# A one-core transformer block: bias tiles loaded in four groups, the position check moved to the table, one difference of the seven products on GpSimd, norm weights by a broadcast load

## The chip, the cores and the metric

The kernel runs on one core of a Trainium2 chip. The metric is device time in microseconds (us) of one execution; three runs of the kernel before gave a median of 908.03 us (907.3 to 908.68). Engines are called by the profile's names: PE is TensorE (PEld its weight loads), DVE is VectorE, ACT is ScalarE, POOL is GpSimd, SP is SyncE, which issues most DMAs. A name with a q (SPq, POOLq) is that engine's sequencer or its DMA queue.

## The reference: what is computed

One transformer block on x (512 x 1024, float32), with three mixers side by side, cut here to its skeleton:

```python
h = rms_norm(x, attn_norm)
proj = h @ w_in                                  # 1024 x 7176, split into 14 parts
o_a = dsa_attention(aq, ak, av, iq, ik, iw, positions, rel_bias)   # top-128 of an index score, T5 bias
o_b = hgrn2_mixer(bq, bf, bi, bg, lower_bounds, hgrn_out_norm)     # gated linear recurrence
o_c = mla_attention(q_nope, q_pe, k_nope, k_pe, v_c)               # causal attention, rope
mixed = g_a * (o_a @ w_up_a) + g_b * (o_b @ w_up_b) + g_c * (o_c @ w_up_c)   # g = sigmoid(gates)
x = x + mixed @ w_out
h = rms_norm(x, ffn_norm)
x = x + (silu(h @ w_gate) * (h @ w_up)) @ w_down # d_ff = 2816
return rms_norm(x, final_norm)
```

In `dsa_attention` a bias `rel_bias[t5_bucket(p_t - p_s)]` is added to the logits of query t and key s. It depends on positions alone. Where positions are consecutive it depends on t - s alone, and the kernel then takes it from a table of 640 distances.

## The kernel before, in words

**Numbers.** A float32 operand is split into two parts of a reduced type (fp32r): `hi` by a cast on ACT, `lo` by a subtraction on DVE, and each product is three matmuls, hi x hi, hi x lo and lo x hi (`mm3`, line 511). A weight tile (`unit`, line 485) is a load into one of three `raw` buffers by SP, a cast `whi` on ACT and a subtraction `wlo` on DVE.

**Products by seven.** The three gates and 18 of the 22 column blocks of the FFN (in pairs, for gate and up) go through `seven` (line 577): a product of a 1024 x 256 weight piece with the 512 columns of h, as 2 x 2 blocks by seven block products in place of eight (Strassen's scheme). It loads two `raw` tiles, the first with x11 and x21 and the second with x12 and x22, and makes four sums of them on DVE: s1 = x21 + x22, s3 = x11 - x21, s2 = s1 - x11, s4 = x12 - s2 (tiles named `sf`). Each of x11, x12, x22, s1, s3, s2 and s4 is split into `sh` and `sl` (`two`) and multiplied in 12 matmuls. It is called 30 times: 12 times for the gates (three branches of four units), 18 times in the FFN.

**Order.** The program text doesn't fix the order on the engines. Every instruction is put down as an `Op` of a `Plan` with its place in the text as its priority, and `Plan.run` (line 258) plays a list schedule ahead of time, with durations from `Plan.cost` (line 225). On each engine the op that can start earliest goes first, then the one with the lower priority number; SP's queue keeps the order of the text. For POOL `cost` takes 147 + 2.105 x n ns for an ordinary operation of n elements per partition, 1500 for a `branch`; a POOL load holds the queue for 1000. What comes out is one fixed order of instructions for each engine, with buffers assigned: among others 33 slots `g` of 128 x 512, three `raw`, eight PSUM banks. On the chip each engine runs its list in order and waits on semaphores for data and for buffers to come free. `plan.gate` (an op) makes later ops wait for that op in the plan; on the chip it is no wait, only a place in the list. `background` (line 938) gives ops a priority behind everything else.

**The start** (lines 451 to 479 and 551 to 572, 704 to 721). Eight warm-up matmuls of an identity run on PE. SP loads the first row tile of x (`xa`, `xb`), then the norm weights as two rows of 2 KB (`gra`, `grb`), then weights. PE broadcasts the rows over the partitions by a matmul with a row of ones, and DVE copies the result to `gna` and `gnb`. `norm_rows` takes the sum of squares of a row tile (for the first tile one half on ACT, one on DVE), its power -1/2 on POOL (`r`), `xn` = x * r * gain on DVE, transposes on PE, and `hT_hi` (ACT) and `hT_lo` (DVE). Four row tiles go by; behind each stands its share of the first projection (`cq`).

**Small loads and the check** (lines 723 to 767). SP loads masks, positions, `line` (0 to 511 on every partition) and small weights. `posr` is the positions as float. The check: the largest of posr - line and the largest of line - posr, each by one reduction over 512 elements on DVE (`jkp`, `ext`), and `odd` = whether they are not each other's negative, that is, whether positions are not consecutive.

**The bias** (lines 881 to 930, 994 to 1006). A matmul makes the table of 640 distances for four heads; POOL writes it to DRAM, `table`, then 128 copies of it, `skew`. `load_bias` reads 16 tiles from `skew` by POOL loads, for each query tile i and head one of 128 x 128(i+1), in the order i = 3, 2, 1, 0. Then a POOL `branch` loads `odd` into a register and computes the bias from the positions if it is set (lines 898 to 917); with the inputs here it is not. `block_mask` adds the causal or top-k mask in the background. All 16 loads and the branch are placed behind the end of the hgrn part (`hgrn_end`, line 1299).

**After that** come the three gated branches (`branch`, line 1270): 2 with `o_c`, 1 with `o_b`, then attention A, which reads the bias tiles, then 0 with `o_a`; each has four units with one call of `seven` and two sets of matmuls for the up-projection. Then the output projection, the FFN and the last norm.

Of the kernel before, what the change touches and what calls it, by code (L numbers as in the profile page):

```python
# [9 lines left out]
F32 = mybir.dt.float32  # L10
# [10 lines left out]
D = 1024  # L21
NF = 22
NG = 33
WARM = 8
PLAIN_GATES = ()
PLAIN = (0, 1, 2, 13)
SLACK = 500.0
# [373 lines left out]
def block_kernel(ctx: ExitStack, tc: tile.TileContext, x, positions, w_in, w_up_a, w_up_b, w_up_c, w_out, mla_q_norm,  # L401
# [25 lines left out]
    def const(shape, dt=F32, name="c"):  # L427
        v = plan.tile(nm("const"), shape, dt, name)
        slots[v.buf.cls] = [(cpool, v.buf.cls)]
        v.buf.left = 1  # L430
        return v
# [21 lines left out]
    P.affine_select(out=ident, in_=ident, compare_op=ALU.not_equal, fill=1.0, base=0, pattern=[[-1, 128]],  # L453
                    channel_multiplier=1)
    warm = bank("t")
    ones = const((128,), F32, "ones")
    P.memset(ones, 1.0)
    for _ in range(WARM):
        PE.matmul(warm[:, 0:128], ident, ident, start=True, stop=True)
    dpool = ctx.enter_context(tc.tile_pool(name="dpool", bufs=1, space=bass.MemoryType.DRAM))  # L460
# [7 lines left out]
    mhalf = const((8,), F32, "mhalf")  # L468
    P.memset(mhalf, -0.5)
    load_x(0)  # L470

    gn = (g(name="gna"), g(name="gnb"))
    gr = (g(name="gra"), g(name="grb"))
    for i in range(2):
        SP.dma_start(gr[i].part(0, 1), attn_norm[0:1, i * 512:(i + 1) * 512])
    for i in range(2):
        pg = bank("t")
        PE.matmul(pg, ones.part(0, 1), gr[i].part(0, 1), start=True, stop=True)
        V.tensor_copy(gn[i], pg)


    class W:
# [68 lines left out]
    def norm_rows(src, gain, dst, t, r=None, plain=None):  # L551

        if r is None:
            ss = st(2, "ss")
            for i in range(2):
                jk = g(name="jk")
                if i and not t and dst is hT:
                    V.tensor_tensor_reduce(out=jk, in0=src[i], in1=src[i], scale=1.0 / 1024, scalar=0.0, op0=ALU.mult,
                                           op1=ALU.add, accum_out=ss[:, i:i + 1])
                else:  # L560
                    A.activation(jk, src[i], AF.Square, scale=1.0 / 32, accum_out=ss[:, i:i + 1])
            r = rms2(ss, "r")
        tt = slice(t * 128, (t + 1) * 128)
        for i in range(2):
            xn = g(name="xn")
            V.scalar_tensor_tensor(xn, src[i], r, gain[i], op0=ALU.mult, op1=ALU.mult)
            pt = bank("t", (128, 4, 128))
            for k in range(4):
                PE.transpose(pt[:, k], xn[:, k * 128:(k + 1) * 128], ident)
            split_ps(dst[0][:, 4 * i:4 * i + 4, tt], dst[1][:, 4 * i:4 * i + 4, tt], pt)  # L570
            if plain:
                A.copy(plain[t // 2][:, 4 * i:4 * i + 4, (t % 2) * 128:(t % 2 + 1) * 128], pt)
# [4 lines left out]
    def seven(wsrc, c0, h, tsum, after=None):  # L577

        t1, t2, t3, t4 = tsum
        x = []  # L580
        for e in range(2):
            raw = plan.tile("raw", (4, 256), F32, "raw")
            SP.dma_start(raw, wsrc[512 * e:512 * e + 512, c0:c0 + 256].rearrange("(k p) c -> p k c", p=128))
            x.append([raw[:, :, 0:128], raw[:, :, 128:256]])

        def two(v):
            plan.gate = after
            hi = plan.tile("g", (4, 128), F32R, "sh", tag="sw")
            lo = plan.tile("g", (4, 128), F32R, "sl", tag="sw")
            A.copy(hi, v)  # L590
            V.tensor_sub(lo, v, f32(hi))
            plan.gate = None
            return hi, lo

        def add(method, a, b):
            plan.gate = after
            o = plan.tile("g", (4, 128), F32, "sf", tag="sf")
            getattr(V, method)(o, a, b)
            plan.gate = None
            return o  # L600

        def prod(o, wt, m, first=True, last=True):
            for k in range(4):
                mm3(o, wt[0][:, k], wt[1][:, k], m[0][:, k], m[1][:, k], first and k == 0, last and k == 3)

        def blk(k, t):
            return h[0][:, k, t], h[1][:, k, t]

        (x11, x21), (x12, x22) = x
        a, b, c = (bank("fs", (128, 2, 256)) for _ in range(3))  # L610
        d = bank("fs")
        prod(a[:, 0], two(x11), blk(ka, lo_t))
        p1 = g((128, 256), name="p1")
        A.copy(p1, a[:, 0])
        prod(a[:, 1], two(x12), blk(kb, lo_t))
        s1 = add("tensor_add", x21, x22)
        s3 = add("tensor_sub", x11, x21)
        s2 = add("tensor_sub", s1, x11)
        prod(b[:, 0], two(x22), t4)
        s4 = add("tensor_sub", x12, s2)  # L620
        prod(c[:, 1], two(s1), t1)
        prod(c[:, 0], two(s3), t3)
        prod(d[:, 0:256], two(s2), t2)
        p16 = g((128, 1, 256), name="p16")
        V.tensor_add(p16[:, 0], p1, d[:, 0:256])
        prod(b[:, 1], two(s4), blk(kb, hi_t))
        u = g((128, 2, 256), name="fu")
        V.tensor_add(p1, p1, a[:, 1])
        V.tensor_add(u, c, p16.to_broadcast([128, 2, 256]))
        o = g((128, 2, 256), name="fv")  # L630
        V.tensor_add(o, u, b)
        V.tensor_add(u[:, 0], u[:, 0], c[:, 1])
        return (p1, o[:, 1]), (o[:, 0], u[:, 0])
# [124 lines left out]
    V.tensor_copy(pos_f, pos_i)  # L758
    posr = g(name="posr")
    V.tensor_copy(posr, posr_i)  # L760

    ext = [const((1,), F32, "ext") for _ in range(2)]
    odd = const((1,), I32, "odd")
    jkp = g(name="jkp")
    for e, u, v in ((ext[0], posr, line), (ext[1], line, posr)):
        V.tensor_tensor_reduce(out=jkp, in0=u, in1=v, scale=1.0, scalar=-3e38, op0=ALU.subtract, op1=ALU.max, accum_out=e)
    V.scalar_tensor_tensor(odd, ext[0], -1.0, ext[1], op0=ALU.mult, op1=ALU.not_equal)
    sncs = g((128, 2, 4, 32), name="sncs")
    sn, cs = sncs[:, 0], sncs[:, 1]
    ang = g((128, 4, 32), name="ang")  # L770
# [110 lines left out]
    def load_bias():  # L881

        b3 = [g(name="bias3") for _ in range(4)]
        b20 = [g(name="bias2") for _ in range(4)]
        b1 = [g((128, 2, 256), name="bias1") for _ in range(2)]
        for h in range(4):
            bias[h, 3], bias[h, 2], bias[h, 0] = b3[h], b20[h][:, 0:384], b20[h][:, 384:512]
            bias[h, 1] = b1[h // 2][:, h % 2]
        keys = [(h, i) for i in (3, 2, 1, 0) for h in range(4)]
        for h, i in keys:  # L890
            S = 128 * (i + 1)
            first = TL * h + 511 - 128 * i
            P.dma_start(bias[h, i], View(skew.buf, np.arange(S), (
                lambda a, first=first, S=S: bass.AP(tensor=a.tensor, offset=a.offset + first,
                                                    ap=[[4 * TL - 1, 128], [1, S]]),)))
        scr = [g(name="scr") for _ in range(4)]

        def general(nc, odd, posr, pos_f, rb, *tiles):
            q = nc.gpsimd
            r = q.value_load(odd[0:1, 0:1])  # L900
            with tc.If(r != 0):
                for i in range(NT):
                    S = 128 * (i + 1)
                    d, w, e, u = (v[:, :S] for v in tiles[:4])
                    q.tensor_scalar(d, posr[:, :S], -1.0, pos_f[:, i:i + 1], op0=ALU.mult, op1=ALU.add)
                    bh = [t for t, k in zip(tiles[4:], keys) if k[1] == i]
                    for h in range(4):
                        q.tensor_scalar(bh[h], d, 1.0, rb[:, 0, h:h + 1], op0=ALU.is_lt, op1=ALU.mult)
                    q.tensor_scalar(w, d, float(BOUNDS[0]), None, op0=ALU.is_ge)
                    for k in range(1, 32):  # L910
                        if k < 31:
                            q.tensor_scalar(e, d, float(BOUNDS[k]), None, op0=ALU.is_ge)
                            q.tensor_tensor(w, w, e, op=ALU.subtract)
                        for h in range(4):
                            q.tensor_scalar(u, w, rb[:, k, h:h + 1], None, op0=ALU.mult)
                            q.tensor_tensor(bh[h], bh[h], u, op=ALU.add)
                        w, e = e, w

        plan.add([("Pool", "branch", (odd, posr, pos_f, rb), dict(
            body=general, outs=scr + [bias[k] for k in keys]))])  # L920

    def block_mask(i):
        S = 128 * (i + 1)
# [62 lines left out]
    for t in range(NT):  # L986
# [3 lines left out]
        A.copy(v, p)  # L990
        vc.append(v)


    rbk = const((4,), F32, "rbk")
    SP.dma_start(rbk.part(0, 32), rel_bias)
# [271 lines left out]

    mixed = [None] * 8

    def branch(n, wu, o, first):  # L1270
        wuu = None
        for u in range(4):
            if u % 2 == 0:
                wuu = unit([(wu[0][:, 256 * u:256 * u + 512], 0)], 4, 512)
            plain = n in PLAIN_GATES
# [20 lines left out]
                    V.tensor_mul(sg, sg, p)  # L1296
                    V.tensor_add(mixed[j], mixed[j], sg)

    plan.gate = hgrn_end
    load_bias()  # L1300
    plan.gate = None
    for i in range(NT):
        background(block_mask, i)
    branch(2, w_up_c, ocT, True)
    branch(1, w_up_b, obT, False)

    oaT = (o8(name="oa_hi"), o8(name="oa_lo"))
# [191 lines left out]
```

## Time and profile before

| | us |
|---|---|
| median of three runs | 908.03 |
| profiled execution | 913.61 |
| span of it, first to last instruction | 911.0 |
| mean granted PE clock | 0.994 |
| bytes moved by DMA | 90.36 MB, mean 99 GB/s |

A row of a timeline reads: start, length, engine, line, operation, tiles written <- tiles read, shapes, count, and in brackets the idle time of that engine before it and who ended it. L397 is the line at which the planned order is emitted, so nearly all instructions carry it and are told apart by their tiles. In a windows row stand the stretch, its length, busy time of PE, PEld, DVE, ACT and POOL (with the number of instructions), the granted PE clock, the share of the DMA engines in use and GB/s. A waits row gives who waited for whom: us in total, times, the longest.

### The profile page before, as it was taken

The page shows a single profiled execution, that of the slowest core. Times are in us where ns is not written, and L with a number is a line of the kernel's source. Part 1 is how long each engine was busy: PE and PEld are TensorE (multiplying, and loading weights), DVE is VectorE, ACT ScalarE, POOL GpSimd, SP SyncE. Part 2 cuts the span into 40 slices and gives each one's busy share as a digit, 9 for nine tenths or more (in the row PEclk, how much of TensorE's full clock was granted, in tenths as well). Part 3 has the DMA queues.
Part 4 walks back from the last instruction along what each step waited for, and adds up shares of the span by engine and source line. Part 5 has one row for each costly group of instructions (what it writes and reads, how often), then busy time and mean ns, then how long its engine had stood idle before and what let it go on. Part 6 is the DMA issues. An engine that isn't in the chain of part 4 may idle for free.

```text
span 911.0 us, 16024 instructions
## 1 busy us (share of the span) xinstructions
PE 890.6 (98%) x6304; PEld 795.1 (87%) x6304; DVE 673.7 (74%) x1382; ACT 440.5 (48%) x915; POOL 27.6 (3%) x51
## 2 busy tenths in 40 slices
PE   9899999999999899999999999999999999999997
PEld 7897878888788899998999878999999999988885
DVE  5566999968866797979649558789996899533335
ACT  6654687333535454537925347454454453422313
POOL 1000000000002200000000000000000000000000
PEclk9999999999999999999999999999999999999999
DMA  7343150333202632334104731323342334341312
GB/s 237 74 116 85 42 151 24 93 92 94 72 26 74 205 94 64 122 96 136 47 5 135 235 112 47 116 71 95 121 132 71 94 101 149 99 139 50 110 49 92
DMA packets 77920, 90.36 MB, mean 99 GB/s; under 512 B 8778, under 2 KB 64238, under 8 KB 77716
## 3 DMA queue, kind: packets, MB, share of 16 engines
q1 hardware_dynamic: 76596, 85.13, 30.8%
q0 software_dynamic: 1104, 3.94, 1.5%
q8 instruction: 49, 0.80, 0.4%
q14 instruction: 27, 0.22, 0.1%
q10 hardware_dynamic: 144, 0.26, 0.1%
HBM read 87.21 MB, written 3.42 MB: 99 GB/s over the span
## 4 chain that ended last, share of the span: by engine, by line
PE 79%; DVE 8%; DMA 7%; ACT 3%; issue 2%; SPq 0%; POOL 0%; POOLq 0%; ACTq 0%; DVEq 0%
PE ps L397 78%; DMA raw<-in_w_in 3%; DMA raw<-in_w_ffn_up 1%; DVE wlo L397 1%; PE ps L1089 1%; DVE sl L397 1%; DVE sf L397 1%; DMA line<-in_consts_f 1%; DMA x2b<-in_x 1%; DMA raw<-in_w_ffn_gate 1%; DVE fu L397 0%; ACT whi L397 0%; DVE quarters_sl L397 0%; DVE p L397 0%; DMA raw<-in_w_up_a 0%
## 5 line engine op out<-in xcount | busy, mean ns | idle before, releaser
L397 DVE TENSOR_TENSOR wlo<-raw,whi 128x1024 fp32r<-128x1024 f32 (+3 forms) x91 | 104.3, 1166 | 47.1 <-ACT whi L397 37.0
L397 ACT CAST whi<-raw 128x1024 fp32r<-128x1024 f32 (+3 forms) x91 | 89.2, 1006 | 56.7 <-DMA raw<-in_w_ffn_up 23.0
L397 PE MATMUL ps<-whi,hT_lo 128*128 128x512 f32 (+3 forms) x160 | 55.5, 349 | 2.3 <-DVE hT_lo L397 2.3
L397 PE MATMUL ps<-whi,hT_hi 128*128 128x512 f32 (+3 forms) x160 | 55.5, 352 | 1.3 <-ACT hT_hi L397 1.3
L397 ACT CAST sh<-sf 128x512 fp32r<-128x512 f32 x75 | 45.6, 619 | 22.7 <-DVE sf L397 19.7
L397 PE MATMUL ps<-wlo,hT_hi 128*128 128x512 f32 (+3 forms) x160 | 55.3, 347 | 0.0
L397 PE MATMUL ps<-hT_hi,wlo 128*128 128x512 f32 x136 | 54.5, 400 | 0.0
L397 PE MATMUL ps<-hT_hi,whi 128*128 128x512 f32 x136 | 54.3, 399 | 0.0
L397 PE MATMUL ps<-hT_lo,whi 128*128 128x512 f32 x136 | 54.1, 398 | 0.0
L397 PE MATMUL ps<-whi,quarters_ah 128*128 128x512 f32 x160 | 53.2, 389 | 0.0
L397 ACT CAST sh<-raw 128x512 fp32r<-128x512 f32 x55 | 33.1, 619 | 39.4 <-DMA raw<-in_w_ffn_gate 16.0
L397 PE MATMUL ps<-tl,sh 128*128 128x256 f32 x176 | 49.8, 283 | 0.0
L397 PE MATMUL ps<-th,sh 128*128 128x256 f32 x176 | 49.8, 283 | 0.0
L397 PE MATMUL ps<-th,sl 128*128 128x256 f32 x164 | 46.4, 283 | 0.0
L397 PE MATMUL ps<-whi,quarters_sl 128*128 128x512 f32 x120 | 40.0, 389 | 0.0
L397 PE MATMUL ps<-h_hi,sh 128*128 128x256 f32 x136 | 38.6, 284 | 0.0
L397 PE MATMUL ps<-h_lo,sh 128*128 128x256 f32 x136 | 38.5, 283 | 0.0
L397 PE MATMUL ps<-hth,sh 128*128 128x256 f32 x132 | 37.6, 286 | 0.0
L397 PE MATMUL ps<-htl,sh 128*128 128x256 f32 x132 | 37.5, 285 | 0.0
L397 PE MATMUL ps<-h_hi,sl 128*128 128x256 f32 x128 | 36.2, 283 | 0.0
L397 PEld LDWEIGHTS ps<-whi,hT_lo 128*128 128x128 f32 x160 | 31.4, 196 | 5.0 <-DVE hT_lo L397 2.6
L397 PEld LDWEIGHTS ps<-whi,hT_hi 128*128 128x128 f32 x160 | 31.3, 197 | 4.9 <-ACT hT_hi L397 2.2
(422 smaller groups left out, 2870.8 us busy)
## 6 DMA issues: line engine op xcount, KB each, us to landing
raw<-in_w_in SPq DMA_DIRECT2D x51, 512.0 KB, 3.7
raw<-in_w_ffn_down SPq DMA_DIRECT2D x22, 512.0 KB, 4.3
raw<-in_w_ffn_gate SPq DMA_DIRECT2D x18, 512.0 KB, 3.6
raw<-in_w_ffn_up SPq DMA_DIRECT2D x18, 512.0 KB, 4.2
raw<-in_w_out SPq DMA_DIRECT2D x8, 512.0 KB, 4.4
raw<-in_w_up_c SPq DMA_DIRECT2D x4, 512.0 KB, 3.7
raw<-in_w_up_b SPq DMA_DIRECT2D x4, 512.0 KB, 3.5
raw<-in_w_up_a SPq DMA_DIRECT2D x4, 512.0 KB, 3.7
```

The lines of the kernel that those rows point to most:

```text
L397: getattr(real[e], method)(*[fix(v) for v in a], **{n: fix(v) for n, v in k.items()})
L1089: nc.tensor.matmul(v[2 * n + i], v[i], v[n + i], start=True, stop=True)
```

## The change

Six edits. (1) `WARM`, the number of warm-up matmuls, goes from 8 to 11. (2) The norm weights come by two loads that read the 2 KB row once for each partition (256 KB each) in place of rows, ones, matmuls and copies. (3) The second square of the first tile goes from DVE to ACT. (4) In `seven`, s3 is made by POOL. (5) The position check goes from its place among the small loads to a place behind the MLA values `vc`, ahead of the table, gated there. (6) `load_bias` becomes a generator: the four loads of one i are placed behind whatever op was last put down before each unit of branch 2 (i = 3 ahead of unit 0, i = 0 ahead of unit 3), the POOL branch behind branch 2, and the masks after it.

```diff
 NG = 33
-WARM = 8
+WARM = 11
 PLAIN_GATES = ()
...
     warm = bank("t")
-    ones = const((128,), F32, "ones")
-    P.memset(ones, 1.0)
     for _ in range(WARM):
...
     load_x(0)
-
     gn = (g(name="gna"), g(name="gnb"))
-    gr = (g(name="gra"), g(name="grb"))
     for i in range(2):
-        SP.dma_start(gr[i].part(0, 1), attn_norm[0:1, i * 512:(i + 1) * 512])
-    for i in range(2):
-        pg = bank("t")
-        PE.matmul(pg, ones.part(0, 1), gr[i].part(0, 1), start=True, stop=True)
-        V.tensor_copy(gn[i], pg)
+        SP.dma_start(gn[i], bcast(attn_norm[0, i * 512:(i + 1) * 512], 512))
 
...
                 jk = g(name="jk")
-                if i and not t and dst is hT:
-                    V.tensor_tensor_reduce(out=jk, in0=src[i], in1=src[i], scale=1.0 / 1024, scalar=0.0, op0=ALU.mult,
-                                           op1=ALU.add, accum_out=ss[:, i:i + 1])
-                else:
-                    A.activation(jk, src[i], AF.Square, scale=1.0 / 32, accum_out=ss[:, i:i + 1])
+                A.activation(jk, src[i], AF.Square, scale=1.0 / 32, accum_out=ss[:, i:i + 1])
             r = rms2(ss, "r")
...
 
-        def add(method, a, b):
+        def add(method, a, b, eng=V):
             plan.gate = after
             o = plan.tile("g", (4, 128), F32, "sf", tag="sf")
-            getattr(V, method)(o, a, b)
+            getattr(eng, method)(o, a, b)
             plan.gate = None
...
         s1 = add("tensor_add", x21, x22)
-        s3 = add("tensor_sub", x11, x21)
+        s3 = add("tensor_sub", x11, x21, P)
         s2 = add("tensor_sub", s1, x11)
...
     V.tensor_copy(posr, posr_i)
-
-    ext = [const((1,), F32, "ext") for _ in range(2)]
-    odd = const((1,), I32, "odd")
-    jkp = g(name="jkp")
-    for e, u, v in ((ext[0], posr, line), (ext[1], line, posr)):
-        V.tensor_tensor_reduce(out=jkp, in0=u, in1=v, scale=1.0, scalar=-3e38, op0=ALU.subtract, op1=ALU.max, accum_out=e)
-    V.scalar_tensor_tensor(odd, ext[0], -1.0, ext[1], op0=ALU.mult, op1=ALU.not_equal)
     sncs = g((128, 2, 4, 32), name="sncs")
...
         keys = [(h, i) for i in (3, 2, 1, 0) for h in range(4)]
-        for h, i in keys:
+        for n, (h, i) in enumerate(keys):
+            if n % 4 == 0:
+                yield
             S = 128 * (i + 1)
...
                                                     ap=[[4 * TL - 1, 128], [1, S]]),)))
+        yield
         scr = [g(name="scr") for _ in range(4)]
...
             body=general, outs=scr + [bias[k] for k in keys]))])
+        yield
 
...
 
+    plan.gate = plan.ops[-1]
+
+    ext = [const((1,), F32, "ext") for _ in range(2)]
+    odd = const((1,), I32, "odd")
+    jkp = g(name="jkp")
+    for e, u, v in ((ext[0], posr, line), (ext[1], line, posr)):
+        V.tensor_tensor_reduce(out=jkp, in0=u, in1=v, scale=1.0, scalar=-3e38, op0=ALU.subtract, op1=ALU.max, accum_out=e)
+    V.scalar_tensor_tensor(odd, ext[0], -1.0, ext[1], op0=ALU.mult, op1=ALU.not_equal)
+    plan.gate = None
 
...
 
-    def branch(n, wu, o, first):
+    def branch(n, wu, o, first, between=None):
         wuu = None
         for u in range(4):
+            if between:
+                plan.gate = plan.ops[-1]
+                next(between)
+                plan.gate = None
             if u % 2 == 0:
...
 
-    plan.gate = hgrn_end
-    load_bias()
+    lb_ = load_bias()
+    next(lb_)
+    branch(2, w_up_c, ocT, True, lb_)
+    plan.gate = plan.ops[-1]
+    next(lb_)
     plan.gate = None
...
         background(block_mask, i)
-    branch(2, w_up_c, ocT, True)
     branch(1, w_up_b, obT, False)
...
```

## The prediction

> **What bounds the kernel now.** I read the page first, then TensorE's waits, then the windows around the two longest ones, then the timeline and the chain of waits inside them.
>
> ```profile
> span 911.0 us, 16024 instructions
> PE 890.6 (98%) x6304; PEld 795.1 (87%) x6304; DVE 673.7 (74%) x1382; ACT 440.5 (48%) x915; POOL 27.6 (3%) x51
> ...
> PE   9899999999999899999999999999999999999997
> ...
> DVE  5566999968866797979649558789996899533335
> ```
>
> TensorE (PE) is busy for 98% of the span. What a change can win is PE's idle time (911.0 - 890.6 = 20 us) and the stretches in which PE runs at half its clock. The longest waits of PE, by who ended them:
>
> ```profile
> PE ps L397 <- ACT sh L397: 2.7, 1, 2.7
> PE ps L397 <- DVE hT_lo L397: 2.3, 1, 2.3
> ```
>
> Both are single events, at 297 and 26.7 us. Windows laid around them (busy time of PE, PEld, DVE, ACT, POOL with instruction counts, then granted clock, DMA share, GB/s):
>
> ```profile
> 24.00:26.60 2.60, 2.00 (x13) 1.24 (x10) 0.22 (x2) 2.58 (x6) 0.00 (x0) 1.00 0.70 187
> 26.60:30.00 3.40, 1.08 (x7) 1.02 (x7) 3.28 (x9) 1.69 (x6) 0.00 (x0) 1.00 0.25 61
> 30.10:33.50 3.40, 3.40 (x13) 3.40 (x12) 2.85 (x15) 1.80 (x3) 0.00 (x0) 0.50 0.00 0
> 33.50:37.00 3.50, 3.50 (x22) 3.50 (x21) 0.69 (x3) 2.33 (x6) 0.00 (x0) 1.00 0.01 2
> ...
> 296.30:299.70 3.40, 1.00 (x5) 0.50 (x3) 0.57 (x2) 0.35 (x1) 0.00 (x0) 1.00 0.96 347
> 299.75:303.10 3.35, 3.08 (x11) 2.79 (x12) 3.35 (x7) 2.96 (x6) 0.00 (x0) 0.50 0.22 46
> ```
>
> Each gap is followed by 3.4 us at a granted clock of 0.50: the same kind of matmul goes through 13 times in 3.4 us, then 22 times in 3.5. So each event costs its gap and another 3.4 x 0.5 = 1.7 us: 2.3 + 1.7 = 4.0 us near 27, 2.7 + 1.7 = 4.4 us near 297. The Trainium skill, "TensorE: Matmul & The Clock Gate" (Part 1), describes the same free-running window of 3413 ns, but asks for an idle gap above about 3.4 us; here gaps of 2.3 and 2.7 us were followed by the drop, so the trace decides. By that rule each event would be worth its gap alone, and the sum below would come out some 2.5 us smaller.
>
> **The position check** (old lines 762 to 767). What holds PE at 26.7:
>
> ```profile
> 26.72 0.69 DVE L397 CUSTOM_DVE_ANT_0 jkp<-posr,line 128x512 f32<-128x512 f32 x1 [2.50 <-DMA line<-in_consts_f]
> ...
> 28.24 1.88 DVE L397 TENSOR_TENSOR hT_lo<-ps,hT_hi 128x512 fp32r<-128x512 f32 x3
> ...
> 28.98 0.45 PE L397 MATMUL ps<-whi,hT_lo 128*128 128x384 f32 x1 [2.31 <-DVE hT_lo L397]
> ```
>
> VectorE (DVE) runs in order. The check's first reduction waits 2.50 us for the load of `line`; behind it are queued the four splits `hT_lo` of the last two row tiles, and PE waits for the first. Moved behind the MLA values, the check no longer stands there, while `line` is loaded as before and has landed long since. The split could then go once ScalarE's `hT_hi` is there, whose own waits in this place are the 0.6 us that PE idles at 24 to 26.6. I take 4.0 us for gap and clock together, bounds 2.0 (the tile behind it is late for its own sake, and the clock still drops) and 4.6 (the 0.6 goes too). At its new place the check is two reductions of 0.69 us and a compare: about 1.5 us of DVE at 120 us, where DVE's strip reads 9 (slices 5 to 8, 91 to 182 us) and PE's reads 9 as well. What fills DVE there is mostly the top-k rounds, which the planner puts at the lowest priority and nobody waits for; if the check falls between a softmax's steps instead, it costs up to 1.5. I take +0.5.
>
> **Norm weights and warm-up** (old lines 455 to 479, 557). The start:
>
> ```profile
> 4.17 0.69 DVE L397 CUSTOM_DVE_ANT_0 jk<-xb 128x512 f32<-128x512 f32 x1 [4.17 <-DMA xb<-in_x]
> ...
> 5.30 0.55 POOL L397 TENSOR_TENSOR r<-ms,mhalf 128x1 f32<-128x1 f32 x1 [3.84 <-DVE ms L397]
> ...
> 6.42 0.83 ACT L397 CAST whi<-raw 128x768 fp32r<-128x768 f32 x1 [2.21 <-DMA raw<-in_w_in]
> ...
> 7.28 0.69 DVE L397 COPY gna<-ps 128x512 f32<-128x512 f32 x1 [2.14 <-PE ps L397]
> 8.08 0.75 DVE L397 SCALAR_TENSOR_TENSOR xn<-xa,r,gna 128x512 f32<-128x512 f32 x1
> 8.49 0.63 ACT L397 ACTIVATE jk<-xa 128x512 f32<-128x512 f32 x1 [0.24 <-DMA xa<-in_x]
> ...
> 10.68 0.69 PE L397 MATMUL ps<-whi,hT_hi 128*128 128x384 f32 x1 [0.68 <-ACT hT_hi L397]
> ```
>
> The factor `r` is there at 5.85, but `xn` starts at 8.08, after the broadcast matmuls and their copy. In their place come two loads of 256 KB, third and fourth in SyncE's queue. Between 4.17 and 8.49 there landed 384 + 384 + 256 KB (two weight tiles and `xa`): 237 KB per us. So the first half of the weights lands about 4.17 + 1.1 = 5.3 and `xn` can start at about 6.0 instead of 8.08. But everything behind the two loads lands 512 / 237 = 2.2 us later: the first weight tile at 8.6 instead of 6.4, cast by 9.4, so the first real matmul goes at about 9.4 instead of 10.68: a gain of 1.3 us, not 2.1. The square that moves from DVE to ScalarE ends at about 5 us as before (`xb` lands at 4.17, and a square takes ScalarE 0.63): nothing. The three more warm-up matmuls run while PE waits for `xn`: nothing, unless they bring the full clock a window sooner, for up to 1.7. What the extra 512 KB does after that:
>
> ```profile
> 9.60:13.00 3.40, 2.73 (x11) 2.20 (x11) 3.40 (x7) 2.35 (x5) 0.17 (x1) 1.00 0.37 92
> 13.00:16.40 3.40, 3.40 (x12) 3.40 (x11) 3.40 (x5) 1.81 (x5) 1.03 (x1) 1.00 0.89 302
> 16.40:20.00 3.60, 3.60 (x25) 3.52 (x25) 1.76 (x5) 3.33 (x10) 0.55 (x1) 1.00 1.08 370
> ```
>
> From 13 to 20 us the DMA engines are full, and the last rows of x come in there. From 9.6 to 13 they are 37% used, because SyncE waits for a weight slot: 0.63 x 3.4 = 2.1 us of room, about what the two loads take. I take -1.3, bounds -3.0 (a clock window too) and +2.2 (no room used).
>
> **Bias tiles in four groups** (old lines 881 to 920, 1299 to 1304). The wait at 297 is for a weight tile:
>
> ```profile
> 291.19 2.26 POOL L397 DMA_DIRECT2D bias<-skew  x4
> ...
> 305.41 0.55 POOL L397 DMA_DIRECT2D bias<-skew  x1 [9.54 <-PE ps L397]
> ```
>
> ```profile
> 292.39 6.88 DMA raw<-in_w_in
> ...
> 299.35 0.63 ACT sh L397
> ```
>
> ```profile
> raw<-in_w_in SPq DMA_DIRECT2D x51, 512.0 KB, 3.7
> ...
> bias<-skew POOLq DMA_DIRECT2D x4, 256.0 KB, 4.2
> ```
>
> That load took 6.88 us where the median of its kind is 3.7, with the DMA engines at 0.96: four bias loads of 256 KB and two of 192 KB stand beside it. Without any it would land at 296.1, before PE runs dry at 297.3. But the plan's gate only orders the queue: the first group, the four of 256 KB, is issued behind the last product of the branch before, and that is the same place. What goes for certain is the two of 192 KB, 384 KB at the window's 347 KB per us: 1.1 us of the gap. A gap of 1.6 in a window of 3.4 may or may not halve the clock. I take -2.0 (1.1 and half of 1.7), bounds 0 and -4.4.
>
> On GpSimd's queue the groups, and the branch behind them, now stand ahead of the differences of later units. A bias load waited 9.54 us there for a slot that PE held. The branch takes from its load of the flag to the instruction after it:
>
> ```profile
> L900 POOLq TENSOR_LOAD <-odd x1: 491/491/491, 315.5 to 315.5; - x1
> ```
>
> ```profile
> L901 POOLq EVENT_SEMAPHORE  x1: 17/17/17, 319.2 to 319.2; - x1
> ```
>
> some 3.8 us, in which a difference queued behind it cannot start, nor ScalarE's cast of it, nor PE's product. The planner counts 1.5. The slot waits follow PE's own progress, so what stands behind them isn't due sooner; I take +0.5 for both, bounds 0 and +2.3 (3.8 - 1.5).
>
> **The difference on GpSimd** (old line 617). It is `x11 - x21`, once for each of 30 products by seven: 12 in the branches, 18 in the FFN. On DVE in the FFN:
>
> ```profile
> 600.00:690.00 90.00, 88.93 (x737) 88.35 (x737) 85.99 (x158) 45.30 (x90) 0.00 (x0) 1.00 0.35 106
> ```
>
> ```profile
> L397 DVE TENSOR_TENSOR sf<-raw 128x512 f32<-128x512 f32 x8 | 5.5, 684 | 0.0
> ```
>
> ```profile
> PE ps L397 <- ACT p L397: 1.1, 2, 0.7
> PE ps L397 <- ACT whi L397: 0.8, 1, 0.8
> ```
>
> In these 90 us nine products go by: 84 matmuls each, 0.121 us a piece (88.93 / 737), so 10.1 us of PE, and 9.55 us of DVE (85.99 / 9). The change takes 0.68 from DVE, which leaves 8.9. But DVE isn't PE's limit yet: in the whole FFN PE waits 1.9 us (the third fence), and so no more than 1.9 can be won. What the difference takes on GpSimd no row shows. Nearest rows:
>
> ```profile
> L397 POOL TENSOR_TENSOR rb<-ms,mhalf 128x4 f32<-128x4 f32 x4 | 4.0, 1012 | 60.7 <-DVE ms L397 60.7
> ...
> L397 POOL MEMSET at<- 128x512 f32 x4 | 2.1, 526 | 96.2 <-DVE kT L397 70.9 <-ACT sm L397 15.7 <-PE ps L397 9.6
> ```
>
> A pass of the same size that only writes takes 0.53; two reads and a write would make three such passes, 1.6 as an estimate from that row. I take 1.2, between the two and the planner's own figure (line 256: 512 x 2.105 + 147 ns). GpSimd is free for it (3%), and its product is the fifth of the seven in the code, so four others, 4 x 12 x 0.121 = 5.8 us of PE, cover its lateness. I take -0.5, bounds -1.9 and, by the second rival, +12.
>
> **Sum.** -4.0 + 0.5 - 1.3 - 2.0 + 0.5 - 0.5 = -6.8 us. The profiled execution took 913.6 (span 911.0 and 2.6 around it), 5.6 more than the median of 908.0; the terms are waits that both have, so 906.8 profiled, and **901.2** as the median. Its own range, from the neighbouring bounds, is 897.5 to 904.5.
>
> **Rivals.** *The start is bound by its loads.* For it: 0.89 and 1.08 of DMA between 13 and 20 us. If the 512 KB does not fit into the free 2.1 us, the last rows of x come 2.2 us later, PE finds the gap again a little further on, and the clock drops again. The start then gives 0 instead of -5.3: 901.2 + 5.3 = 906.5.
>
> *The difference collides with DVE.* For it: DVE has only 10.1 - 8.9 = 1.2 us to spare in each FFN product, and 11 of its operations there read two SBUF tiles. If it is held while GpSimd reads, each difference costs DVE its length and the one operation that GpSimd itself waits for, 1.2 + 0.68 = 1.9 us; from 1.2 on DVE is the bound. That is 0.7 us x 18 = 12.6 us, less the 0.5 counted: 901.2 + 13 = 914; a half of it still gives 908. Against it: GpSimd is used 3% of the time in this trace, so no row shows a collision. The Trainium skill, "SBUF — State Buffer" (Who interferes with whom), does say that a DVE instruction with two SBUF inputs contends with a GpSimd instruction that reads SBUF, and that the second blocks until the first is done. By that rule the time would be this rival's 914; no row here tests it, which is why the rival has a chance of its own.
>
> *The groups change nothing*, since the first MB is issued at the same moment: the wait at 297 stays whole, 901.2 + 2.0 = 903.2, and the branch on GpSimd may take 1 more: 904.
>
> **How the numbers follow.** Forecast 0.60, loads 0.17, collision 0.13, groups 0.10. A measurement can tell about 0.2% from no change, 1.8 us: faster is below 906.2, slower above 909.8. The forecast and the last rival are faster; of the first rival 0.45 faster, 0.4 same, 0.15 slower; of the collision most is slower. Together 0.75 faster, 0.11 same, 0.14 slower. The range runs from 895 (start and wait both at their best bounds) to 910 (the collision at a third, or the loads with the check's cost); beyond it is what is left of the collision and of a reordered plan.
>
> **What would show it.** Right: PE has no wait above 1 us for `hT_lo` before 35 us, no half-clock stretch near 30, `xn` starts near 6.0 and the first product near 9.4; the raw load at the start of the first branch lands in 5 to 6 us. Wrong: DVE operations of 128x512 with two SBUF inputs well over 0.69 us in the FFN, `sf` on POOL over 1.7, PE waiting for `sh` there; or the same gap at 25 to 35 us ended by `xa` or `xb`.

## The result, and the profile after

Four runs of the changed kernel gave a median of 920.15 us (919.3 to 920.63), four of the kernel before beside it 908.36 (907.3 to 909.93): a ratio of 1.0127 with a 95% interval of [1.0110, 1.0145], so 11.8 us slower. 901.2 was forecast, with a range up to 910. The profiled execution took 919.3 us. The two profiled executions differ by 5.7 us only, because that of before lay 5.6 above its median and this one 0.9 below.

The head of its page and the strips of PE and DVE:

```profile
span 917.5 us, 16114 instructions
...
PE 890.1 (97%) x6306; PEld 794.8 (87%) x6306; DVE 671.3 (73%) x1348; ACT 443.1 (48%) x919; POOL 74.8 (8%) x80
...
PE   7899999999999999999999999999999999999997
...
DVE  4566999968866778987695468789897899542335
```

PE's busy time is as before (890.6), the span is 6.5 us longer: PE waits more. DVE lost 34 instructions (30 differences, the two copies, a square with its readout), which at 0.68 us should be some 23 us of busy time; it lost 2.4. POOL took 47 us more.

PE's waits (us in total, times, longest), the longest first:

```profile
PE ps L397 <- ACT p L397: 7.0, 7, 1.3
PE ps L397 <- DVE xn L397: 3.5, 3, 1.5
PE ps L397 <- ACT hT_hi L397: 2.2, 3, 1.0
PE ps L397 <- DVE hT_lo L397: 1.6, 1, 1.6
```

The wait of 2.7 for `sh` at 297 is gone from the top. The wait for `hT_lo` is still there, 1.6 us at 27, and in front is what stood at 1.1 us in two waits in the whole of before: `p`, a step of the products by seven.

The FFN window and windows around the start, with the columns of the windows before (busy time of PE, PEld, DVE, ACT, POOL; granted clock, DMA share, GB/s):

```profile
24.00:26.60 2.60, 1.82 (x16) 1.58 (x15) 1.59 (x9) 1.83 (x6) 0.00 (x0) 1.00 0.80 185
26.60:30.00 3.40, 1.78 (x7) 1.46 (x7) 3.26 (x10) 3.35 (x8) 0.00 (x0) 0.86 0.22 52
29.06:32.47 3.41, 3.41 (x12) 3.41 (x12) 2.02 (x8) 2.98 (x11) 0.00 (x0) 0.50 0.00 0
...
600.00:690.00 90.00, 86.06 (x709) 85.08 (x707) 81.98 (x146) 42.14 (x83) 11.77 (x8) 1.00 0.34 101
```

In 90 us of the FFN 709 matmuls go by where there were 737: 28 x 0.121 = 3.4 us lost, as an estimate. DVE is busy for 82 of the 90 us, less than before, so it isn't the bound by its load. POOL takes 11.77 us for 8 operations, 1.5 each.

The same operations by tile, with least, median and largest duration in ns. Before:

```profile
L397 DVE TENSOR_TENSOR sl<-sf,sh x39: 681/686/694, 286.5 to 772.9; 128x512 fp32r<-128x512 f32 x39
L397 DVE TENSOR_TENSOR sf<-raw x30: 680/684/691, 284.6 to 761.5; 128x512 f32<-128x512 f32 x30
```

After:

```profile
L397 DVE TENSOR_TENSOR sl<-sf,sh x50: 673/682/1784, 286.9 to 778.8; 128x512 fp32r<-128x512 f32 x50
...
L397 POOL TENSOR_TENSOR sf<-raw x30: 1273/1396/3520, 284.5 to 762.7; 128x512 f32<-128x512 f32 x30
```

On DVE the difference took 0.68 us to within 2%. On POOL it takes 1.27 at the least and up to 3.5, and DVE operations that never passed 0.70 reach 1.78. In all 21 DVE operations of this size with two SBUF inputs took over 0.8 us (called held below), 14.7 us more than 0.685 each; before there was none. One such pair in the timeline:

```profile
284.48 1.29 POOL L397 TENSOR_TENSOR sf<-raw 128x512 f32<-128x512 f32 x1 [25.84 <-PE ps L397]
...
285.05 1.27 DVE L397 TENSOR_TENSOR sl<-raw,sh 128x512 fp32r<-128x512 f32 x1
```

DVE's operation starts 0.57 us into POOL's, which ends at 285.77, and is done at 286.32, 0.55 after that: it did most of its work once POOL was done. All 21 held operations started during a difference on POOL and ended 0.545 to 0.554 us behind it, however much of it had been left: that is how an exclusive hold reads, not two engines that share a rate. Operations of DVE that read a PSUM bank were not held: 29 of them ran at least in part beside a difference, and those of 128x512 took 0.67 to 0.69 as ever. The reverse shows too: two stretches of the chain of work that ended last (start, length, what):

```profile
391.01 3.53 POOL sf L397
394.55 0.02 issue
394.57 0.62 ACT sh L397
395.19 0.53 ACT quarters_sl L397
...
687.23 2.28 POOL sf L397
689.51 0.02 issue
689.53 0.02 ACT sh L397
689.56 0.50 issue
690.06 0.37 ACT p L397
```

A difference that takes 3.5 or 2.3 us holds up ScalarE's cast of it. ScalarE runs in order, so `p` (the copy of a finished product out of PSUM) waits behind the cast, and PE waits for `p`'s bank. The first of the two stretches cost the clock as well: PE waited 1.3 us in it, and 3.4 us at half clock followed, where before shows 1.00 in both windows:

```profile
394.10:397.70 3.60, 2.04 (x15) 1.63 (x14) 1.96 (x4) 1.70 (x3) 0.43 (x1) 1.00 0.00 0
397.70:401.10 3.40, 3.40 (x18) 3.40 (x18) 3.37 (x7) 0.85 (x3) 0.00 (x0) 0.50 0.76 213
```

### The profile page after: what moved, and what is told of

It is laid out like the page before. It is cut to its first block, busy times and chain, and to the rows that moved or that the text cites. A ratio compares the mean times of both kernels' runs of the same rounds, so it can differ in the third digit from the quotient of the medians.

```text
span 917.5 us, 16114 instructions
## 1 busy us (share of the span) xinstructions
PE 890.1 (97%) x6306; PEld 794.8 (87%) x6306; DVE 671.3 (73%) x1348; ACT 443.1 (48%) x919; POOL 74.8 (8%) x80
## 4 chain that ended last, share of the span: by engine, by line
PE 69%; DVE 12%; DMA 8%; ACT 6%; issue 3%; POOL 1%; SPq 0%; POOLq 0%; DVEq 0%; ACTq 0%
PE ps L397 68%; DMA raw<-in_w_ffn_up 4%; DVE sl L397 3%; DMA raw<-in_w_in 2%; DVE sf L397 1%; ACT sm L397 1%; DVE wlo L397 1%; PE ps L1083 1%; ACT whi L397 1%; DVE quarters_sl L397 1%; DMA x2b<-in_x 1%; ACT L397 1%; POOL sf L397 1%; DVE p L397 1%; DVE fu L397 1%
## 5 line engine op out<-in xcount | busy, mean ns | idle before, releaser
L397 POOL TENSOR_TENSOR sf<-raw 128x512 f32<-128x512 f32 x30 | 48.2, 1606 | 347.6 <-DMA raw<-in_w_in 81.4
L397 PE MATMUL ps<-th,sl 128*128 128x256 f32 x208 | 58.9, 283 | 0.0
L397 ACT CAST sh<-raw 128x512 fp32r<-128x512 f32 x50 | 30.1, 619 | 33.0 <-DMA raw<-in_w_in 11.4
L397 PE MATMUL ps<-hth,quarters_sl 128*128 128x256 f32 x160 | 39.0, 291 | 1.6 <-ACT quarters_sl L397 1.3
L397 PEld LDWEIGHTS ps<-th,sl 128*128 128x128 f32 x208 | 39.9, 192 | 0.0
L397 DVE TENSOR_TENSOR sl<-sf,sh 128x512 fp32r<-128x512 f32 x50 | 36.9, 753 | 2.8 <-ACT sh L397 2.6
L397 PE MATMUL ps<-h_hi,sh 128*128 128x256 f32 x120 | 34.4, 287 | 2.0 <-ACT p L397 1.9
L397 PE MATMUL ps<-hth,sh 128*128 128x256 f32 x124 | 35.7, 288 | 0.0
```

What stands on the lines that cost most here:

```text
L397: getattr(real[e], method)(*[fix(v) for v in a], **{n: fix(v) for n, v in k.items()})
```

## Experiments

The theory after this reading: the difference on POOL is the loss; it collides with DVE, each holds the other, and the late operation reaches PE through ScalarE's queue. Its rivals: the new order of the plan; the price of the operation alone (1.3 in place of 0.68); and the start. "Before" below is measured on the same chip beside each batch (medians 910.63, 910.74, 911.32, 911.24); the batches ran on different chips, so ratios are compared and not times. All ratios are to before, with 95% intervals.

**ctl_before.** The kernel before, for a second profile of it.

> The kernel before, unchanged, profiled once more. If its profiled execution of 913.6 us, 5.3 above the median, was that long because of where the clock's 3.4 us windows fell, this one shows fewer than two half-clock stretches and a span some 2 to 5 us under 911.0. If profiling itself costs 5 us, it shows 911 again with the same two stretches near 30 and 300 us.

914.68 us profiled, span 912.2. PE's wait for `hT_lo` is there again, near 26; the one for `sh` at 297 is 1.3 us instead of 2.7, with no half clock behind it. The half clock behind the first lasted 6.8 us, from 27.2 to 34.0, instead of 3.4. So both events on which the forecast counted differ from one execution to the next, and neither reading that was expected fits whole: the span is no shorter, though one of the stretches is gone.

**undo_sub.** The kernel after, difference back on DVE.

```diff
-        s3 = add("tensor_sub", x11, x21, P)
+        s3 = add("tensor_sub", x11, x21)
```

> The changed kernel with the difference x11 - x21 back on VectorE, all else as changed. Theory (GpSimd's difference and its collisions with VectorE cost the time): 907 to 909 us, ratio to the kernel before 0.998 to 1.001, and no wait of PE above 1 us after 600 us. Rival (the bias groups, the start or the moved check cost it): stays above 915.

Ratio 1.0033 [1.0014, 1.0052]. Of the 1.27% in after, 0.94% (8.6 us) goes with this line alone. The 0.33% that stays is more than was expected and is taken up in the sum below. The FFN window is as it was before:

```profile
600.00:690.00 90.00, 88.99 (x738) 88.38 (x737) 85.83 (x158) 45.31 (x90) 0.00 (x0) 1.00 0.37 108
```

**only_sub.** The kernel before, the difference alone on POOL (the same line, the other way).

> The kernel before with the difference on GpSimd alone. Theory: 917 to 921 us, ratio 1.010 to 1.014, VectorE operations of 128x512 stretched to 1.2 to 1.8 us whenever a difference runs on GpSimd. Rival (cost elsewhere): within 2 us of 908.

Ratio 1.0077 [1.0047, 1.0107]; 19 DVE operations held, 17.1 us in sum. That is the theory's sign, at less than the 1.010 to 1.014 expected.

**only_start.** The kernel before with the two broadcast loads, 11 warm-up matmuls and the square on ScalarE.

> The kernel before with the norm weights by broadcast loads, 11 warm-up matmuls and the square on ScalarE alone. In the changed kernel's trace the first projection's tiles are done 2.95, 0.18, -0.35 and -0.18 us later than in the kernel before, so the start's loads eat what the matmuls gave: 908 us, within 1.5. Rival (the start lost what the moved check gained): 910 to 914.

Ratio 1.0018 [1.0001, 1.0035]: no gain, a small loss.

**moved_pool.** Before's plan and order kept on every engine; only when the planned list is emitted are the 30 differences given to POOL.

```diff
         s3 = add("tensor_sub", x11, x21)
+        plan.ops[-1].choices[0][3]["moved"] = True
...
+            if k.pop("moved", None):
+                e = "Pool"
```

> The plan of the kernel before, with the order on every engine kept, and only the 30 differences issued to GpSimd in place of VectorE. Theory (the collision and GpSimd's length cost the time on the chip): slower by 0.6 to 1.1%, like the difference alone (1.0077), with VectorE operations held to 1.2 to 1.8 us. Rival (the planner, told another engine and another length, makes a worse order): within 0.2% of before.

Ratio 1.0068 [1.0042, 1.0094]. With no other instruction out of its place the loss is nearly that of only_sub, and 27 operations are held by 21.0 us: the new order isn't the cause.

**moved_dve.** The reverse: after's order, with the differences emitted on DVE.

> The plan of the changed kernel, order kept, and only the 30 differences issued to VectorE in place of GpSimd. Theory: the 0.9% between the changed kernel and the one with the difference undone goes away, ratio to before 1.002 to 1.005. Rival (the order): it stays at 1.010 to 1.014.

Ratio 1.0149 [1.0114, 1.0184], worse than after. All DVE operations are at 0.68 to 0.69 again, so no collision is left, but another wait has come in (the second row; in before it is 0.9 us):

```profile
L399 DVE TENSOR_TENSOR sf<-raw x30: 681/691/695, 286.3 to 765.8; 128x512 f32<-128x512 f32 x30
```

```profile
DVE sf L399 <- DMA raw<-in_w_ffn_up: 10.0, 11, 1.5
```

In the places that the plan chose for POOL, DVE stands in its order and waits for weight loads. By its expectation this is the rival's outcome, the order. But the wait that came in is 3.5 us in after: the run says that an order made for one assignment of engines is bad for the other, and tests neither the collision nor the order as after has it.

**dummy_sub and dummy_set.** Before's order with the difference on DVE, and after each one an operation on POOL whose result nobody reads: a subtraction of the same size with two reads, or a copy of one element and a memset of the same size that only writes.

```diff
+    def extra(nc, s3):
+        nc.gpsimd.tensor_sub(xb_, s3, s3)
```

```diff
+    def extra(nc, s3):
+        nc.gpsimd.tensor_copy(xb_[:, 0, 0:1], s3[:, 0, 0:1])
+        nc.gpsimd.memset(xb_, 0.0)
```

> The kernel before, order kept, with its difference on VectorE, and after each one a subtraction of the same size on GpSimd that reads it twice and writes a tile nobody reads: 30 operations more than the reference needs. Nobody waits for them. Theory (VectorE is held while GpSimd reads): VectorE operations with two SBUF inputs are held some 20 times by 0.7 us on average, VectorE saves nothing, and the time goes up by 0.5 to 1.2%. Rival (PE waits because the difference itself comes late from GpSimd): within 0.2% of before, since nothing needed is late.

> As the run with the unused subtraction, but in its place on GpSimd a copy of one element of the difference and a memset of 128x512, which writes and reads nothing: again nobody needs it. Theory: no VectorE operation is held and the time is within 0.2% of before. Rival (any work on GpSimd next to VectorE costs): as the unused subtraction.

Ratios 1.0047 [1.0029, 1.0066] and 1.0016 [0.9990, 1.0041]. In dummy_sub nothing waits for POOL, and yet 24 DVE operations are held, by 15.6 us; in dummy_set none. The two intervals overlap, so it is the held operations and not the times that tell the two apart; PE's wait for `p` goes with them, 5.2 us in dummy_sub and 1.4 in dummy_set. By tile, dummy_sub:

```profile
L398 DVE TENSOR_TENSOR sl<-sf,sh x39: 674/681/1476, 285.7 to 776.0; 128x512 fp32r<-128x512 f32 x39
...
L1481 POOL TENSOR_TENSOR xtra<-sf x30: 1040/1356/6177, 283.9 to 765.0; 128x512 f32<-128x512 f32 x30
```

dummy_set:

```profile
L398 DVE TENSOR_TENSOR sl<-sf,sh x39: 677/683/693, 285.5 to 771.0; 128x512 fp32r<-128x512 f32 x39
...
L1481 POOL COPY xtra<-sf x30: 182/512/5330, 284.3 to 760.2; 128x1 f32<-128x1 f32 x30
L1482 POOL MEMSET xtra<- x30: 524/527/536, 284.6 to 761.4; 128x512 f32 x30
```

So it is POOL's reading that collides: the memset takes 527 ns each time and holds nobody, though 21 of the 30 ran at least in part beside a DVE operation with two SBUF inputs, while a copy of one element took up to 5.3 us. (Spans on POOL are rough in this profile; that no DVE operation is held doesn't rest on them.) Over all profiles PE waits 4.7 to 9.7 us for `p` in the five in which a subtraction of this size runs on POOL, and 0.7 to 2.8 in the others, moved_dve apart (8.1). The collision alone costs about 0.47% (4.3 us); the rest up to 0.7 to 0.9% comes where somebody waits for the late difference (moved_pool and only_sub above dummy_sub; the intervals touch, so this share is likely, not shown).

**only_check and check_tail.** The kernel before with the check alone moved; and with, besides, everything of the rope table and of the HGRN bounds gated behind the last split.

```diff
         norm_rows(xt[t], gn, hT, t)
+        split_end = plan.ops[-1]
...
+    plan.gate = split_end
     pos_f = const((4,), F32, "pos_f")
...
     V.tensor_scalar(om, lb, -1.0, 1.0, op0=ALU.mult, op1=ALU.add)
+    plan.gate = None
```

> The kernel before with the position check alone moved. Theory A (the next late wait takes its place): DVE's queue ahead of the splits now holds the subtraction of lbl, which waits for its load, and the rope table's steps; PE's gap near 26 us stays between 1.3 and 2.6 us and a half-clock stretch still follows, so the time is within 1.5 us of before (ratio 0.9985 to 1.0015). Prediction's step: the gap goes, no half clock before 35 us, ratio 0.9955 (-4 us).

> As only_check, but everything of the rope table and of the HGRN bounds is gated behind the last split of the normed rows, so that nothing that waits for a late load stands ahead of the splits on DVE or ahead of the high halves on ScalarE. Theory A: only now does the gap near 26 go (below 0.8 us, and the half-clock stretch with it): 2 to 4 us faster, ratio 0.9955 to 0.998. Rival B (the gap is ScalarE's and the transposes' own latency, nothing in the queues): the gap stays above 1.3 us, ratio 1.000. In both the rope table, later by 4 us, must not be what PE waits for next near 45 to 60 us; if it is, that wait shows there.

Ratios 0.9982 [0.9962, 1.0002] and 0.9942 [0.9914, 0.9969]. In only_check the gap of PE is still 2.4 us, and 3.4 us at half clock follow it:

```profile
25.25 0.16 DVE L397 TENSOR_TENSOR lbe<-lbl 128x4 f32<-128x4 f32 x1 [1.49 <-DMA lbl<-in_hgrn_lb_logits]
...
26.48 2.48 DVE L397 TENSOR_TENSOR hT_lo<-ps,hT_hi 128x512 fp32r<-128x512 f32 x4
...
27.21 0.44 PE L397 MATMUL ps<-whi,hT_lo 128*128 128x384 f32 x1 [2.36 <-DVE hT_lo L397]
```

In check_tail the split comes as soon as ScalarE's half is there, PE's longest wait between 20 and 36 us is 0.5, and the clock stays full (windows):

```profile
23.74 2.48 DVE L397 TENSOR_TENSOR hT_lo<-ps,hT_hi 128x512 fp32r<-128x512 f32 x4 [2.30 <-ACT hT_hi L397]
```

```profile
22.60:26.20 3.60, 3.03 (x19) 2.47 (x18) 2.46 (x5) 3.54 (x9) 0.00 (x0) 1.00 0.80 180
26.20:29.60 3.40, 3.40 (x21) 3.40 (x20) 3.14 (x19) 1.83 (x6) 0.00 (x0) 1.00 0.07 14
```

The 4 us that the forecast saw there exist (5.3 us by the ratio, interval 2.8 to 7.8). Moving the check alone wins 1.6 us at the middle of its interval, which still holds zero; moving all that waits for late loads wins them.

**only_bias and tail_bias.** The bias groups alone, and on top of check_tail.

> The kernel before with the bias groups alone. Prediction's step: the weight tile at the start of the first branch lands earlier, the gap of 1.5 to 2.7 us near 297 shrinks by 1.1 us or more, -2.0 us, ratio 0.998. Rival (the groups change nothing, as the first MB is issued at the same place): 1.000. The gap near 297 differed between two profiles of the same kernel (2.7 and 1.45), so the ratio decides more than the gap.

> check_tail and only_bias together, without the difference on GpSimd and without the broadcast loads of the norm weights: the two gains lie in different stages and should add, -4 to -6 us, ratio 0.9935 to 0.996; if one of the two is nothing by itself, the ratio is the other's.

Ratios 0.9988 [0.9967, 1.0010] and 0.9959 [0.9938, 0.9980]: nothing that can be told from zero, and on top of check_tail none either. The weight tile at the start of the branch still takes 6.2 us (chain of only_bias) and PE waits 2.0 us for it:

```profile
289.43 6.21 DMA raw<-in_w_in
```

**start_loads, tail_all, tail_sub.** The two broadcast loads alone; after with the difference on DVE and the gate of check_tail; check_tail with the difference on POOL.

> The kernel before with the two broadcast loads alone (8 warm-up matmuls, the square still on DVE). Theory A (the loads cost): in the run with all three edits of the start the two loads landed 4.1 us behind the first rows of x and the first weight tile 2.9 us later than before; that is all the start's cost, so the weight tile lands near 9.3 us again and the ratio is 1.001 to 1.0035. Rival B (the other two edits cost: 11 warm-up matmuls or the square on ScalarE): the weight tile is as late, but the ratio is 1.000 or below, since the broadcast by two matmuls and copies is saved.

> The kernel after with the difference back on DVE and with the rope table and the HGRN bounds gated behind the last split. It differs from the run tail_bias by the start's three edits alone. If the costs add: 0.9959 + 0.0018 = 0.998 (0.996 to 1.000). If the start costs more in this company, as the 1.0033 of after with the difference on DVE hints (its parts alone add to 0.9988): 1.000 to 1.003.

> check_tail with the difference on GpSimd. If the collision costs what it cost alone (+0.8%), 0.9942 + 0.0077 = 1.002 (0.999 to 1.005), with 18 to 25 DVE operations held over 0.8 us and FFN stalls of 1 to 1.7 us. If the cost in after (1.0127 against 1.0033 without it, +0.9%) was raised by something else in after: below 1.000.

Ratios 1.0002 [0.9984, 1.0020], 0.9972 [0.9955, 0.9990] and 1.0060 [1.0039, 1.0081]. The loads alone don't differ from before: the interval holds both times that were expected. The weight tile is late in it too, cast from 9.93 us on. The three edits of the start neither win nor clearly lose (tail_all against tail_bias: +0.13%, less than the intervals), and the difference costs the good start 1.2% (1.0060 against 0.9942, from two batches), more than the 1.002 that was expected, with 20 operations held by 16.3 us. The best version that ran is check_tail, 906.81 us beside 911.32 for before.

## Why the prediction was wrong, step by step

**The difference on POOL: the failed step.** "I take 1.2 ... I take -0.5, bounds -1.9 and, by the second rival, +12." The estimate of one operation was nearly right (1.27 at the least, median 1.40, mean 1.61), the term was not: it is +6 to +11 us (0.68% with the order kept, 0.77% alone, 0.94% taken out of after, 1.2% with a mended start). What failed is the sentence that "four others ... cover its lateness": that cover is one of PE's work, but neither engine is free to run beside the other. The collision, a rival at 0.13, is what happened: 914 was its time, 920 was measured. That 914 came out low isn't the collision's doing: the rival's own term was +12.6, above what was measured, and 914 still counted the other gains of 6.3 us, most of which did not come. Its mechanism was half right. DVE did not become the bound; it is busy for 82 of 90 us. The loss is lateness: a difference of 2 to 3.5 us, or a held operation of DVE, feeds ScalarE late, and `p` and PE queue behind. (That a late `sl` also frees a weight buffer late is likely: two chains of work in after, at 640 and 661 us, go from `sl` through a weight load to `sh`, `p` and PE. It was not tested.) "GpSimd is used 3% of the time in this trace, so no row shows a collision" is not so. Most POOL rows of before are no evidence: memsets, which dummy_set shows not to collide, and operations on 1 to 4 elements that ran beside no DVE operation with two SBUF inputs or began before it. One row does show the collision:

```profile
12.66 0.95 DVE L397 TENSOR_TENSOR wlo<-raw,whi 128x768 fp32r<-128x768 f32 x1
...
12.83 1.20 POOL L397 TENSOR_TENSOR r<-ms,mhalf 128x1 f32<-128x1 f32 x1 [6.97 <-DVE ms L397]
```

The seven other `r` took 0.55 to 0.57 us. This one, on one element per partition, began 0.17 us into a DVE operation with two SBUF inputs and took 1.20, ending 0.41 behind that one's end; ctl_before has the same pair with the same 1.20. It shows POOL held by DVE, not yet DVE by POOL. The Trainium skill, "SBUF — State Buffer" (Who interferes with whom), states that a DVE instruction with two SBUF inputs and a GpSimd instruction that reads SBUF exclude each other. These runs agree: 0.68 became up to 1.78 us, and the end of the held operation lay 0.55 us behind the end of POOL's.

**The position check: the second failed step.** "The split could then go once ScalarE's hT_hi is there" names ScalarE's own 0.6 us as what is late next, but did not look at the queue behind the check. In after:

```profile
25.45 0.16 DVE L397 TENSOR_TENSOR lbe<-lbl 128x4 f32<-128x4 f32 x1 [0.91 <-DMA lbl<-in_hgrn_lb_logits]
...
25.65 0.21 ACT L397 ACTIVATE lbe<-lbe 128x4 f32<-128x4 f32 x1 [0.77 <-DVE lbe L397]
25.76 2.03 ACT L397 CAST hT_hi<-ps 128x512 fp32r<-128x512 f32 x4
...
27.88 1.28 DVE L397 TENSOR_TENSOR hT_lo<-ps,hT_hi 128x512 fp32r<-128x512 f32 x2
28.62 0.44 PE L397 MATMUL ps<-whi,hT_lo 128*128 128x384 f32 x1 [1.62 <-DVE hT_lo L397]
```

`lbl`, loaded right behind `line`, takes its place on DVE; ScalarE's exponential of it now stands ahead of `hT_hi`; and the steps of the rope table fill DVE until 27.88. The term was -1.6 us (0.9982, interval from -3.5 to +0.2) instead of -3.5 with the check's own +0.5, and the half-clock stretch stayed (29.06 to 32.47 above). check_tail shows that the size of the stall was read rightly.

**The norm weights.** Forecast -1.3, `xn` at 6.0 and the first product at 9.4. The start of after:

```profile
6.58 0.75 DVE L397 SCALAR_TENSOR_TENSOR xn<-xa,r,gna 128x512 f32<-128x512 f32 x1 [1.63 <-DMA gna<-in_attn_norm]
...
8.31 0.75 DVE L397 SCALAR_TENSOR_TENSOR xn<-xb,r,gnb 128x512 f32<-128x512 f32 x1 [0.98 <-DMA gnb<-in_attn_norm]
...
9.25 0.83 ACT L397 CAST whi<-raw 128x768 fp32r<-128x768 f32 x1 [4.50 <-DMA raw<-in_w_in]
9.99 0.58 ACT L397 CAST hT_hi<-ps 128x512 fp32r<-128x512 f32 x1
...
10.62 0.69 PE L397 MATMUL ps<-whi,hT_hi 128*128 128x384 f32 x1 [0.39 <-ACT hT_hi L397]
```

The two loads were worked out at 237 KB per us, the pace of weight tiles: 2.2 us. The second half of the weights was there at 8.31, some 4 us behind `xb` (there by 4.03). The weight tile came at 9.25 instead of 6.42, 2.8 us later and not 2.2, and the first product at 10.62 instead of 10.68. Of the 1.2 us between the forecast's 9.4 and 10.62, 0.65 are the weight tile's (9.25 and not 8.6); the rest is the cast `hT_hi`, which stands behind the weight cast on ScalarE and which the forecast didn't count. So the gain is nil: the runs give +0.2 us (start_loads) and +1.6 (only_start), with intervals from -1.5 to +3.2.

**The bias groups.** Forecast -2.0, bounds 0 and -4.4. Measured -1.1 with an interval from -3.0 to +0.9. The 1.1 us of the two loads that "goes for certain" did not go: the gap was 2.0 us and the load 6.21 in only_bias, between the two profiles of before (1.3 and 2.7 us; 5.47 and 6.88). The last rival, that the groups change nothing, fits; its branch on POOL costs nothing that shows.

**The clock.** Each gap was priced at itself and 1.7 us. In only_bias a gap of 2.3 us for `hT_lo` had no half-clock stretch behind it, in before the same gap had one; in ctl_before a gap of 1.8 us had 6.8 us behind it, in after one of 1.3 us had 3.4. The price holds only for some executions, and the length of the gap alone doesn't tell which.

**The sum.** By the runs: difference +8.6, start +1.6, check -1.6, bias -1.1, together +7.5 of the 11.8. The remaining 4 us stay open. tail_all against tail_bias shows no extra cost of the start beside the other edits, and the intervals of the four terms, 1.6 to 2.4 us each, can hold most of it.

## What to carry to other kernels

An idle GpSimd is no free place for elementwise work beside a busy VectorE: an operation there that reads SBUF and one on VectorE with two SBUF inputs waited for each other in these runs, and both came out late though neither engine was full. Before costing such a move, count the two-input VectorE operations around it, compare the longest of equal small GpSimd operations with the shortest (here 1.20 and 0.55 us, before the change), and test the collision with an operation whose result nobody reads. When a waiting instruction is moved out of an in-order queue, read the next instructions in that queue and what they wait for; the gain comes when the last of them is gone.

## What the runs showed of the hardware

- A GpSimd copy of a single element took 182 to 5330 ns beside VectorE's back-to-back work (median 512). The longest stood through nine operations of VectorE, and all over 200 ns ended 0.04 to 0.05 us behind one with two SBUF inputs. So GpSimd's wait doesn't depend on how much it reads; none of these copies held VectorE.
- A write-only memset of 128x512 on GpSimd took 524 to 536 ns thirty times, right behind those copies, and held nothing.
- A load that reads one 2 KB row once per partition is slower than its 256 KB suggest: the two took some 4 us together behind the first rows of x, and the weight tile of 384 KB right behind them came 0.94 us after the second (8.31 and 9.25).
- The granted clock can be shown as 1.00 where PE runs at half pace. In before, products of 384 columns start 0.32 us apart up to 16.2 us and 0.17 apart from 16.5 on, and the prediction's two rows around that time (12 matmuls in 3.4 us, then 25 in 3.6) both show 1.00. So the early rows of that column are not to be trusted.
